# Mixing's value, gate and half u and the memory's keys by token with 512 weight columns moving, roots by token, and a filler of 32 bytes

## The chip, the cores and the metric

The kernel runs on one core of one Trainium2 chip. The metric is the device time of one execution in microseconds (us). The kernel before took 2160.71 us, the median of 3 runs (2157.63 to 2162.42).

## The reference

One layer of a streaming encoder in float32, 256 tokens of width D = 2048, with 256 memory tokens:

```
x += 1/2 * (silu(h W_gate) * (h W_up)) W_out          h = rms(x), hidden width 5632
p = rms(x) @ W_mix_in -> [value | gate | u | v]       1024 columns each
  A = silu(LayerNorm(causal depthwise conv31(value * sigmoid(gate))))
  B = gelu(u) * (masked W_s (LN gelu(v)) + b)         over chunks of 128 positions, 8 groups
x += concat(rms(A), rms(B)) @ W_mix_out
x += softmax(q k^T / sqrt(512)) v ... @ W_o           4 heads; q from rms(x), k and v from rms(mem)
x += 1/2 * SwiGLU_2(rms(x));  out = rms(x)
```

All products of weights with activations need nearly float32 precision. The norms' root of a token is a factor per token, so it can be applied after the product with the weights.

## The kernel before

**Precision.** Every weight and activation is split in two parts of type float32r, hi and lo (x = hi + lo). A product is three matmuls: hi with hi, hi with lo and lo with hi. `weights` (lines 97 to 109) brings a chunk of 128 x 1024 weights: one DMA of 512 KB on SP's queue into a `raw` tile (4 buffers), a copy on ScalarE that makes hi (line 104) and a subtraction on VectorE that makes lo (line 105), both into an `hl` tile (3 buffers). Each chunk is 4 KB in every partition.

**Two shapes of product.** Activations lie by feature: x_hl is [128 features, 16 feature tiles, hi and lo, 256 tokens]. In `gemm_t` with joint=True (`product_joint`, lines 120 to 125) a weight tile of 128 x 128 is the stationary operand and 256 tokens move: three matmuls with 256 columns for each weight tile; the result is by feature. In `gemm_n` (lines 152 to 169) 128 tokens of x_hl are the stationary operand and 512 weight columns move, six matmuls for each 128 x 512 weights (two token halves), and the result is by token, in two PSUM tiles acc[0] and acc[1]. So 128 x 1024 weights are 24 matmuls with 256 columns or 12 with 512. PSUM has 6 buffers of `acc` and 2 of `aux`.

**Stages.** First FFN: `swiglu_in` (lines 267 to 308) in 11 groups of 512 hidden columns by token, whose results are turned to features with transposes on PE (`turn`, 4 transposes a call, two calls a group) into hA (tiles 0 to 15, in the pool `big`) and hB (tiles 16 to 43, in the pool `ffn1`); its output by `gemm_n` in 4 groups (44 feature tiles each: 16 of hA, 28 of hB), turned by `joins` (lines 371 to 386), which adds to x and makes the next x_hl. Mixing (lines 456 to 528): value and gate for 8 column tiles by `gemm_t`, then the half v by `gemm_n`; the memory's keys (16 tiles, lines 586 to 588) and the half u (8 tiles, lines 592 to 599) by `gemm_t`; the memory's values by `gemm_n`. Then mixing's output, attention, and the second FFN like the first, with x2 for the result by token and a last output group in another order (lines 836 to 849).

**Order.** Small work goes beside the matmuls: `put` appends parts with a cost to `later`, and `beside(per)` after each chunk takes parts until a budget of `per` us is spent (lines 80 to 90). The 8 x 31 taps of the convolution (0.4 us of budget each) are such parts, as are the preparation of the memory's activations m_hl and the gate's norms. The argument `between` is a list of calls, here turns, of which one is taken after a chunk, from feature tile k0 = 4 on. The program's order is then rearranged for each engine by the planner of the TileContext, which simulates the engines.

**Roots.** `rms_rows` (line 215) gives the root of each token along the free axis in all partitions, by a product with ones; `rms_cols` (line 220) gives it by token in partitions. r_x and r_m are by rows: r_x multiplies value, gate and u, r_m multiplies the attention's scores over the memory tokens (line 669). r_t and r_mt are by token.

**Where tiles lie.** Pools follow one another in each partition, with tiles rounded up to 32 bytes. The pool `big` holds x_hl, hA, m_hl, y_hl and o_hl in two buffers that begin at bytes 20,032 and 52,800 (313 x 64 and 825 x 64). The pool `st` of small tiles takes 12,256 bytes from 132,672 to 144,928. There `ffn1`, later `mid` and the second FFN's pool begin, each with its first tile: hB begins at 144,928 (2264 x 64 + 32) in both FFNs. `st` holds r_m and r_x with 1,024 bytes each.

## Time and profile before

| | us |
|---|---|
| median of 3 runs | 2160.71 |
| lowest and highest | 2157.63, 2162.42 |
| the profiled execution | 2159.74 |
| its span, first to last instruction | 2157.9 |
| TensorE (PE) busy | 2137.3 |
| VectorE (DVE) busy | 1301.8 |
| ScalarE (ACT) busy | 996.7 |
| mean granted TensorE clock | 0.999 |

The span is cut into stages by what PE reads: value and gate from 750.6 to 846.0 us, the half v to 889.5, the keys to 985.2, the half u to 1031.3, the memory's values to 1120.2, mixing's output to 1209.2. PE's instructions overlap: the next one starts long before the listed end of the last. So a stream of matmuls is measured from start to start, a listed duration (0.28 or 0.39 us) is not what it costs, and an engine that is busy 99% may still do the same work in less time.

### The profile page before, as it was taken

The page shows a single profiled execution, that of the slowest core. Times are in us where ns is not written, and L with a number is a line of the kernel's source. Part 1 is how long each engine was busy: PE and PEld are TensorE (multiplying, and loading weights), DVE is VectorE, ACT ScalarE, POOL GpSimd, SP SyncE. Part 2 cuts the span into 40 slices and gives each one's busy share as a digit, 9 for nine tenths or more (in the row PEclk, how much of TensorE's full clock was granted, in tenths as well). Part 3 has the DMA queues.
Part 4 walks back from the last instruction along what each step waited for, and adds up shares of the span by engine and source line. Part 5 has one row for each costly group of instructions (what it writes and reads, how often), then busy time and mean ns, then how long its engine had stood idle before and what let it go on. Part 6 is the DMA issues. An engine that isn't in the chain of part 4 may idle for free.

```text
span 2157.9 us, 27852 instructions
## 1 busy us (share of the span) xinstructions
PE 2137.3 (99%) x10844; PEld 1814.8 (84%) x10844; DVE 1301.8 (60%) x1673; ACT 996.7 (46%) x1232; POOL 13.3 (1%) x23
## 2 busy tenths in 40 slices
PE   8999999999999999999999999999999999999998
PEld 6788888888888899999888888888888888888886
DVE  4655445555554489888897666776644545444444
ACT  5544444444444454534575454544444444443443
POOL 0000000000000000000000000000000000000000
PEclk9999999999999999999999999999999999999999
DMA  8766666666666676656666653666666666666664
GB/s 272 228 186 193 188 191 181 194 188 190 186 186 186 186 243 195 186 176 184 187 185 194 187 157 114 200 194 185 189 192 188 192 182 192 191 206 192 188 192 149
DMA packets 113605, 409.92 MB, mean 190 GB/s; under 512 B 12736, under 2 KB 12864, under 8 KB 113344
## 3 DMA queue, kind: packets, MB, share of 16 engines
q1 hardware_dynamic: 113184, 407.35, 62.7%
q8 instruction: 85, 1.39, 0.3%
q10 hardware_dynamic: 288, 0.79, 0.1%
q14 instruction: 48, 0.39, 0.0%
HBM read 405.99 MB, written 2.10 MB: 189 GB/s over the span
## 4 chain that ended last, share of the span: by engine, by line
PE 95%; DMA 2%; DVE 1%; ACT 1%; issue 1%; SPq 0%; DVEq 0%; ACTq 0%
PE acc L262 14%; PE acc L258 14%; PE acc L259 14%; PE acc L165 9%; PE acc L163 9%; PE acc L164 9%; PE acc L117 8%; PE acc L118 4%; PE acc L123 3%; PE acc L124 3%; PE acc L125 3%; PE acc L832 1%; PE acc L834 1%; PE acc L833 1%; PE aux L288 1%; DMA raw<-in_x 1%
## 5 line engine op out<-in xcount | busy, mean ns | idle before, releaser
L105 DVE TENSOR_TENSOR hl<-raw,hl 128x1024 fp32r<-128x1024 f32 x751 | 916.4, 1222 | 783.0 <-ACT hl L104 780.7
L104 ACT CAST hl<-raw 128x1024 fp32r<-128x1024 f32 x751 | 783.0, 1046 | 1014.2 <-PE acc L262 506.9
L259 PE MATMUL acc<-hl,x_hl 128*128 128x512 f32 x1408 | 446.7, 392 | 0.5 <-DVE hl L105 0.5
L262 PE MATMUL acc<-hl,x_hl 128*128 128x512 f32 x1408 | 441.6, 390 | 0.0
L258 PE MATMUL acc<-hl,x_hl 128*128 128x512 f32 x1408 | 395.3, 393 | 9.6 <-ACT hl L104 8.0
L258 PEld LDWEIGHTS acc<-hl,x_hl 128*128 128x128 f32 x1408 | 261.7, 188 | 62.5 <-ACT hl L104 8.4
L262 PEld LDWEIGHTS acc<-hl,x_hl 128*128 128x128 f32 x1408 | 264.9, 188 | 55.5
L259 PEld LDWEIGHTS acc<-hl,x_hl 128*128 128x128 f32 x1408 | 263.2, 188 | 54.9 <-DVE hl L105 1.0
L165 PE MATMUL acc<-hl,hB 128*128 128x512 f32 x392 | 155.1, 396 | 0.0
L164 PE MATMUL acc<-hl,hB 128*128 128x512 f32 x392 | 154.5, 394 | 0.0
L163 PE MATMUL acc<-hl,hB 128*128 128x512 f32 x392 | 139.2, 395 | 0.0
L125 PE MATMUL acc<-x_hl,hl 128*128 128x256 f32 x384 | 108.7, 285 | 0.3
L123 PE MATMUL acc<-x_hl,hl 128*128 128x256 f32 x384 | 108.7, 284 | 0.2 <-ACT hl L104 0.2
L124 PE MATMUL acc<-x_hl,hl 128*128 128x256 f32 x384 | 108.4, 283 | 0.0
L117 PE MATMUL acc<-x_hl,hl 128*128 128x512 f32 x256 | 90.6, 396 | 0.0
L117 PE MATMUL acc<-o_hl,hl 128*128 128x512 f32 x256 | 89.0, 394 | 0.0
L117 PE MATMUL acc<-y_hl,hl 128*128 128x512 f32 x256 | 89.0, 394 | 0.0
L165 PEld LDWEIGHTS acc<-hl,hB 128*128 128x128 f32 x392 | 73.6, 188 | 18.1
L164 PEld LDWEIGHTS acc<-hl,hB 128*128 128x128 f32 x392 | 73.5, 188 | 17.9
L163 PEld LDWEIGHTS acc<-hl,hB 128*128 128x128 f32 x392 | 73.4, 187 | 17.9
L164 PE MATMUL acc<-hl,hA 128*128 128x512 f32 x224 | 87.7, 391 | 0.0
L165 PE MATMUL acc<-hl,hA 128*128 128x512 f32 x224 | 87.3, 390 | 0.0
(225 smaller groups left out, 2644.6 us busy)
## 6 DMA issues: line engine op xcount, KB each, us to landing
raw<-in_ffn_w_in SPq DMA_DIRECT2D x352, 512.0 KB, 3.7
raw<-in_ffn_w_out SPq DMA_DIRECT2D x176, 512.0 KB, 3.7
raw<-in_w_mix_in SPq DMA_DIRECT2D x48, 512.0 KB, 4.5
raw<-in_w_k SPq DMA_DIRECT2D x32, 512.0 KB, 4.1
raw<-in_w_v SPq DMA_DIRECT2D x32, 512.0 KB, 4.3
raw<-in_w_mix_out SPq DMA_DIRECT2D x32, 512.0 KB, 4.5
raw<-in_w_q SPq DMA_DIRECT2D x32, 512.0 KB, 3.9
raw<-in_w_o SPq DMA_DIRECT2D x29, 512.0 KB, 4.5
```

Of the source, the lines that this page charges most:

```text
L104: nc.scalar.copy(out=hl[:, 0, :size], in_=raw[:, :size])
L105: newest[0] = nc.vector.tensor_tensor(out=hl[:, 1, :size], in0=raw[:, :size], in1=hl[:, 0, :size].bitcast(F32), op=ALU.subtract)
L117: nc.tensor.matmul(acc, lhsT=w_hi, rhs=x_hl, start=first, stop=False, skip_group_check=True)
L123: nc.tensor.matmul(d, lhsT=w_hi, rhs=x_hl[:, 0], start=first, stop=False, skip_group_check=True)
L124: nc.tensor.matmul(d, lhsT=w_hi, rhs=x_hl[:, 1], start=False, stop=False, skip_group_check=True)
L125: nc.tensor.matmul(d, lhsT=w_lo, rhs=x_hl[:, 0], start=False, stop=last, skip_group_check=True)
L163: nc.tensor.matmul(acc[t], lhsT=x[:, 0, s], rhs=hi[:, k], start=k0 + k == 0, stop=False)
L164: nc.tensor.matmul(acc[t], lhsT=x[:, 0, s], rhs=lo[:, k], start=False, stop=False)
L165: nc.tensor.matmul(acc[t], lhsT=x[:, 1, s], rhs=hi[:, k], start=False, stop=k0 + k == nk - 1)
L258: nc.tensor.matmul(acc[t][g], lhsT=x[:, 0, s], rhs=hi[:, c], start=first, stop=False)
L259: nc.tensor.matmul(acc[t][g], lhsT=x[:, 0, s], rhs=lo[:, c], start=False, stop=False)
L262: nc.tensor.matmul(acc[t][g], lhsT=x[:, 1, s], rhs=hi[:, c], start=False, stop=last)
```

## The change

Value and gate are now laid out side by side: a group of 512 moving columns has 256 of the value and 256 of the gate (4 groups). The half u (2 groups) and the keys (4 groups) also go through `gemm_n` with 512 columns. Their results by token are finished by token (sigmoid, gelu or a plain copy with the token's root as the scale) into a tile o, and turned to features by `turning`, a helper made out of `joins`: 4 transposes into one `aux` tile and a function that takes it from there. The turns are taken between chunks, from k0 = 4 on, in value and gate from k0 = 2 on. The last turns of the first FFN's output are no longer taken at once but between the first chunks of value and gate. The budget `per` is 1.35 in all these groups (1.0, 1.3 and 0.9 before). load_gate and memory_parts stand ahead of a group instead of behind a column tile. r_x by rows and r_m by rows go; the keys carry the memory's root r_mt, and the scores go to the maximum and the exponential without a product. An unused tile of 32 bytes, to_64, is the first in `st`.

```diff
@@ -73,6 +73,9 @@
     pa = ctx.enter_context(tc.tile_pool(name="pa", bufs=2, space=bass.MemoryType.PSUM))
 
 
+    st.tile([P, 8], F32, name="to_64")
+
+
     later = deque()
     budget = [0.0]
     newest = [None]
@@ -149,7 +152,7 @@
                     between.pop(0)()
         return accs
 
-    def gemm_n(w, x_hl, per=0.0, between=None):
+    def gemm_n(w, x_hl, per=0.0, between=None, after=4):
 
         acc = [ps.tile([P, 2, 256], F32, name="acc").rearrange("p a b -> p (a b)") for _ in range(2)]
         nk = w.shape[1]
@@ -163,7 +166,7 @@
                     nc.tensor.matmul(acc[t], lhsT=x[:, 0, s], rhs=hi[:, k], start=k0 + k == 0, stop=False)
                     nc.tensor.matmul(acc[t], lhsT=x[:, 0, s], rhs=lo[:, k], start=False, stop=False)
                     nc.tensor.matmul(acc[t], lhsT=x[:, 1, s], rhs=hi[:, k], start=False, stop=k0 + k == nk - 1)
-            if between and k0 >= 4:
+            if between and k0 >= after:
                 between.pop(0)()
             beside(per)
         return acc
@@ -244,6 +247,18 @@
             )
         gained(x_hl, f, xT[:, f], col(norm, f))
         square_into(ss, xT[:, f], f == 0)
+
+    def turning(o, c, sink):
+
+        def go():
+            tp = pa.tile([P, 2, T], F32, name="aux")
+            for k in range(2):
+                for t in range(2):
+                    nc.tensor.transpose(
+                        out=tp[:, k, t * P:(t + 1) * P], in_=o[:, t, c + k * P:c + (k + 1) * P], identity=ident
+                    )
+            sink(tp)
+        return go
 
 
     G = 512
@@ -361,22 +376,15 @@
         put(1.4, *[memory_squares(c) for c in range(4)])
         turns = swiglu_in(pool, x_hl, lambda: r_x, a["ffn1_w_in"], hA, hB, first_group, 1.4)
         finish()
-        r_m = rms_rows(sm, D, "r_m")
         r_mt = rms_cols(sm, D, "r_mt")
 
 
         x_hl = gained_tile("mix_norm")
         ss = st.tile([P, T], F32, name="ss", bufs=2)
 
-        def joins(f, o, c):
-
-            def go():
-                tp = pa.tile([P, 2, T], F32, name="aux")
-                for k in range(2):
-                    for t in range(2):
-                        nc.tensor.transpose(
-                            out=tp[:, k, t * P:(t + 1) * P], in_=o[:, t, c + k * P:c + (k + 1) * P], identity=ident
-                        )
+        def joins(f):
+
+            def go(tp):
                 nc.vector.scalar_tensor_tensor(
                     out=xT[:, f:f + 2], in0=tp, scalar=0.5, in1=xT[:, f:f + 2], op0=ALU.mult, op1=ALU.add
                 )
@@ -390,9 +398,7 @@
             o = pool.tile([P, 2, G], F32, name="h", bufs=2)
             for t in range(2):
                 nc.scalar.copy(out=o[:, t], in_=acc[t])
-            turns += [joins(4 * n + 2 * i, o, 2 * i * P) for i in range(2)]
-        while turns:
-            turns.pop(0)()
+            turns += [turning(o, 2 * i * P, joins(4 * n + 2 * i)) for i in range(2)]
 
 
     with tc.tile_pool(name="mid", bufs=1) as mid:
@@ -453,28 +459,33 @@
                         nc.vector.tensor_tensor(out=mu, in0=mu, in1=y[:, j], op=ALU.add)
                 return go
 
-            for j in range(NCT):
-                ws = [a["w_mix_in"][j], a["w_mix_in"][NCT + j]]
-                if j == 0:
-                    accs = ahead(ws, lambda k: x_hl[:, k], per=1.0, joint=True)
-                    r_x = rms_rows(ss, D, "r_x")
+            def gated_input(n):
+
+                def go(tp):
+                    for i in range(2):
+                        j = 2 * n + i
+                        pad = pool.tile([P, PAD + T], F32, name="pad", bufs=6)
+                        half = pool.tile([P, T], F32, name="half", bufs=2)
+                        nc.gpsimd.memset(pad[:, 0:PAD], 0.0)
+                        nc.scalar.copy(out=pad[:, PAD:], in_=tp[:, i])
+                        put(0.4, *[tap(j, pad, i, half) for i in range(TAPS)])
+                        put(0.7, conv_sum(j, half))
+                return go
+
+            for n in range(NCT // 2):
+                load_gate(n)
+                later.appendleft((1.6, memory_parts(n)))
+                acc = gemm_n(a["w_mix_vg"][n], lambda k: x_hl[:, k], per=1.35, between=turns, after=2)
+                if n == 0:
                     r_t = rms_cols(ss, D, "r_t")
-                else:
-                    accs = [gemm_t(w, lambda k: x_hl[:, k], per=1.0, joint=True) for w in ws]
-                tv = ev.tile([P, T], F32, name="tg")
-                tg = ev.tile([P, T], F32, name="tu")
-                nc.vector.tensor_tensor(out=tg, in0=accs[1][:, 0], in1=r_x, op=ALU.mult)
-                nc.scalar.activation(out=tg, in_=tg, func=AF.Sigmoid)
-                nc.vector.tensor_tensor(out=tv, in0=accs[0][:, 0], in1=r_x, op=ALU.mult)
-                pad = pool.tile([P, PAD + T], F32, name="pad", bufs=6)
-                half = pool.tile([P, T], F32, name="half", bufs=2)
-                nc.gpsimd.memset(pad[:, 0:PAD], 0.0)
-                nc.vector.tensor_tensor(out=pad[:, PAD:], in0=tv, in1=tg, op=ALU.mult)
-                put(0.4, *[tap(j, pad, i, half) for i in range(TAPS)])
-                put(0.7, conv_sum(j, half))
-                if j < 4:
-                    load_gate(j)
-                    later.appendleft((1.6, memory_parts(j)))
+                o = pool.tile([P, 2, T], F32, name="o", tag="o", bufs=2)
+                for t in range(2):
+                    tg = ev.tile([P, T], F32, name="tu")
+                    nc.scalar.activation(out=tg, in_=acc[t][:, T:], func=AF.Sigmoid, scale=r_t[:, t:t + 1])
+                    nc.vector.scalar_tensor_tensor(
+                        out=o[:, t], in0=acc[t][:, :T], scalar=r_t[:, t:t + 1], in1=tg, op0=ALU.mult, op1=ALU.mult
+                    )
+                turns.append(turning(o, 0, gated_input(n)))
 
 
             c_state = {}
@@ -522,7 +533,7 @@
 
             vs = pool.tile([P, 2, CC], F32, name="vs")
             for n in range(2):
-                acc = gemm_n(a["w_mix_v"][n], lambda k: x_hl[:, k], per=1.35)
+                acc = gemm_n(a["w_mix_v"][n], lambda k: x_hl[:, k], per=1.35, between=turns)
                 for t in range(2):
                     nc.scalar.activation(
                         out=vs[:, t, n * 512:(n + 1) * 512], in_=acc[t], func=AF.Gelu, scale=r_t[:, t:t + 1]
@@ -583,20 +594,35 @@
             put(3.2, conv_rms)
 
 
-            for f in range(KD):
-                acc = gemm_t(a["w_k"][f], lambda k: m_hl[:, k], per=1.3, joint=True)
-                nc.scalar.copy(out=kT[:, f], in_=acc[:, 0])
+            def keys(f):
+                return lambda tp: nc.scalar.copy(out=kT[:, f:f + 2], in_=tp)
+
+            for n in range(HEADS):
+                acc = gemm_n(a["w_k"][n], lambda k: m_hl[:, k], per=1.35, between=turns)
+                o = pool.tile([P, 2, G], F32, name="o", tag="o", bufs=2)
+                for t in range(2):
+                    nc.scalar.activation(out=o[:, t], in_=acc[t], func=AF.Copy, scale=r_mt[:, t:t + 1])
+                turns += [turning(o, 2 * i * P, keys(4 * n + 2 * i)) for i in range(2)]
 
 
             sg = st.tile([P, T], F32, name="sg")
-            for j in range(NCT):
-                tu = ev.tile([P, T], F32, name="tu")
-                acc = gemm_t(a["w_mix_in"][2 * NCT + j], lambda k: x_hl[:, k], per=0.9, joint=True)
-                nc.vector.tensor_tensor(out=tu, in0=acc[:, 0], in1=r_x, op=ALU.mult)
-                nc.scalar.activation(out=tu, in_=tu, func=AF.Gelu)
-                z = g_state["z"][:, j].rearrange("p n i -> p (n i)")
-                nc.vector.tensor_tensor(out=z, in0=z, in1=tu, op=ALU.mult)
-                square_into(sg, z, j == 0)
+
+            def gating(f):
+                def go(tp):
+                    z = g_state["z"][:, f:f + 2].rearrange("p j n i -> p j (n i)")
+                    nc.vector.tensor_tensor(out=z, in0=z, in1=tp, op=ALU.mult)
+                    for i in range(2):
+                        square_into(sg, z[:, i], f + i == 0)
+                return go
+
+            for n in range(2):
+                acc = gemm_n(a["w_mix_u"][n], lambda k: x_hl[:, k], per=1.35, between=turns)
+                o = pool.tile([P, 2, G], F32, name="o", tag="o", bufs=2)
+                for t in range(2):
+                    nc.scalar.activation(out=o[:, t], in_=acc[t], func=AF.Gelu, scale=r_t[:, t:t + 1])
+                turns += [turning(o, 2 * i * P, gating(4 * n + 2 * i)) for i in range(2)]
+            while turns:
+                turns.pop(0)()
 
             y_hl = big.tile([P, KD, 2, T], F32R, name="y_hl", tag="S")
 
@@ -666,14 +692,13 @@
                     for d in range(KH):
                         product_joint(acc, q_hl[:, d, 0, s], q_hl[:, d, 1, s], k_hl[:, d], d == 0, d == KH - 1)
                     e = pool.tile([P, M], F32, name="e", bufs=4)
-                    nc.vector.tensor_tensor(out=e, in0=acc[:, 0], in1=r_m, op=ALU.mult)
                     mx = st.tile([P, 1], F32, name="mx", bufs=2)
                     sm = st.tile([P, 1], F32, name="sum", bufs=2)
-                    nc.vector.reduce_max(out=mx, in_=e, axis=AX.X)
+                    nc.vector.reduce_max(out=mx, in_=acc[:, 0], axis=AX.X)
                     nc.vector.tensor_scalar(
                         out=mx, in0=mx, scalar1=r_t[:, t:t + 1], scalar2=-1.0, op0=ALU.mult, op1=ALU.mult
                     )
-                    nc.scalar.activation(out=e, in_=e, func=AF.Exp, scale=r_t[:, t:t + 1], bias=mx, accum_out=sm)
+                    nc.scalar.activation(out=e, in_=acc[:, 0], func=AF.Exp, scale=r_t[:, t:t + 1], bias=mx, accum_out=sm)
                     nc.vector.reciprocal(out=sm, in_=sm)
                     nc.vector.tensor_scalar(out=e, in0=e, scalar1=sm, scalar2=None, op0=ALU.mult)
                     pr.append(e)
@@ -878,11 +903,13 @@
         a[name] = np.ascontiguousarray(w.transpose(3, 1, 0, 2, 4).reshape(F // 512, P, KD, 1024))
     a["ffn1_w_out"] = _tiled(g["ffn1_w_out"][0], 512)
     a["ffn2_w_out"] = _tiled(g["ffn2_w_out"][0], 512)
-    a["w_mix_in"] = _tiled(g["w_mix_in"][0][:, :3 * CC], P)
+    w = g["w_mix_in"][0][:, :2 * CC].reshape(KD, P, 2, CC // 256, 256)
+    a["w_mix_vg"] = np.ascontiguousarray(w.transpose(3, 1, 0, 2, 4).reshape(CC // 256, P, KD, 512))
+    a["w_mix_u"] = _tiled(g["w_mix_in"][0][:, 2 * CC:3 * CC], 512)
     a["w_mix_v"] = _tiled(g["w_mix_in"][0][:, 3 * CC:], 512)
     a["w_mix_out"] = _tiled(g["w_mix_out"][0], P)
     a["w_q"] = _tiled(g["w_q"][0], P)
-    a["w_k"] = _tiled(g["w_kv"][0][:, :D], P)
+    a["w_k"] = _tiled(g["w_kv"][0][:, :D], 512)
     a["w_v"] = _tiled(g["w_kv"][0][:, D:], 512)
     a["w_o"] = _tiled(g["w_o"][0], P)
     a["sgu_wT"] = np.ascontiguousarray(g["sgu_w"][0].transpose(2, 0, 1))
```

## Rows read from the trace of the kernel before

**Rows 1.** The page: busy time by engine (part 1) and the chain by engine (part 4).

```profile
PE 2137.3 (99%) x10844; PEld 1814.8 (84%) x10844; DVE 1301.8 (60%) x1673; ACT 996.7 (46%) x1232; POOL 13.3 (1%) x23
...
PE 95%; DMA 2%; DVE 1%; ACT 1%; issue 1%; SPq 0%; DVEq 0%; ACTq 0%
```

**Rows 2.** Stretches: length; PE, PEld, DVE, ACT, POOL busy; PEclk, DMA share, GB/s.

```profile
750.60:846.00 95.40, 94.94 (x784) 94.08 (x783) 81.91 (x149) 48.30 (x69) 1.05 (x8) 1.00 0.70 222
846.00:889.50 43.50, 43.50 (x194) 36.04 (x193) 39.86 (x71) 20.05 (x21) 0.12 (x1) 1.00 0.63 191
889.50:985.20 95.70, 95.70 (x802) 95.66 (x802) 81.41 (x147) 42.87 (x56) 0.00 (x0) 1.00 0.59 177
...
1209.20:1338.70 129.50, 128.42 (x798) 114.45 (x797) 83.32 (x149) 66.75 (x119) 0.00 (x0) 1.00 0.49 144
```

**Rows 3.** Waits of PE: who was waited for, total us, times, longest.

```profile
PE acc L258 <- ACT hl L104: 8.0, 2, 7.6
PE acc L258 <- ACT h L274: 1.6, 1, 1.6
```

**Rows 4.** PE's timeline (start us, us): the half u's first matmul and its successor stage.

```profile
985.18 0.28 PE L123 MATMUL acc<-x_hl,hl 128*128 128x256 f32 x1
...
1031.26 0.40 PE L163 MATMUL acc<-hl,m_hl 128*128 128x512 f32 x1
```

**Rows 5.** PE's timeline: first matmul of the other half, first one of the keys.

```profile
845.99 0.40 PE L163 MATMUL acc<-hl,x_hl 128*128 128x512 f32 x1
...
889.54 0.28 PE L123 MATMUL acc<-m_hl,hl 128*128 128x256 f32 x1
```

**Rows 6.** PE's groups by form: names, shapes, count, busy us, mean ns, idle before.

```profile
L123 PE MATMUL acc<-x_hl,hl 128*128 128x256 f32 x384 | 108.7, 284 | 0.2 <-ACT hl L104 0.2
```

**Rows 7.** PE's timeline: first transposes in two successive groups of the first FFN.

```profile
107.08 0.38 PE L288 MATMUL aux<-ident,h 128*128 128x128 f32 x2
...
151.57 0.38 PE L288 MATMUL aux<-ident,h 128*128 128x128 f32 x2
```

**Rows 8.** PE's timeline: mixing's root by rows, then its root by token.

```profile
766.13 0.59 PE L212 MATMUL aux<-ss,ones 128*128 128x256 f32 x2
766.56 0.50 PE L223 MATMUL aux<-ones,ss 128*128 128x1 f32 x4
```

**Rows 9.** PE's timeline, second FFN's output: where hA begins, hB, hA again.

```profile
1965.96 0.39 PE L163 MATMUL acc<-hl,hA 128*128 128x512 f32 x1
...
1987.73 0.39 PE L163 MATMUL acc<-hl,hB 128*128 128x512 f32 x1
...
2026.92 0.62 PE L163 MATMUL acc<-hl,hA 128*128 128x512 f32 x2
```

**Rows 10.** PE's groups by form with hB as the stationary operand.

```profile
L165 PE MATMUL acc<-hl,hB 128*128 128x512 f32 x392 | 155.1, 396 | 0.0
...
L833 PE MATMUL acc<-hl,hB 128*128 128x512 f32 x40 | 15.8, 395 | 0.0
```

**Rows 11.** ScalarE's groups by form, 750.6 to 1120.2 us.

```profile
L621 ACT ACTIVATE vv<-acc,r_mt 128x512 f32<-128x512 f32 x7 | 4.8, 684 | 1.7 <-PE acc L165 1.7
```

**Rows 12.** VectorE's groups by form, 750.6 to 1120.2 us.

```profile
L105 DVE TENSOR_TENSOR hl<-raw,hl 128x1024 fp32r<-128x1024 f32 x128 | 156.6, 1223 | 40.8 <-ACT hl L104 39.2
L442 DVE SCALAR_TENSOR_TENSOR y<-pad,pv,y 128x256 f32<-128x256 f32 x120 | 57.6, 480 | 0.0
```

**Rows 13.** VectorE's groups by form, 1209.2 to 1415.1 us.

```profile
L669 DVE TENSOR_TENSOR e<-aux,r_m 128x256 f32<-128x256 f32 x8 | 3.4, 421 | 2.4 <-PE aux L125 2.3
```

**Rows 14.** Timeline of SP's queue (DMA issues) where mixing begins.

```profile
736.37 11.53 SPq L101 DMA_DIRECT2D raw<-in_w_mix_in  x5
...
754.57 0.33 SPq L408 DMA_DIRECT2D wT<-in_sgu_wT  x1
```

**Rows 15.** Timeline of ScalarE and of VectorE: the first value and gate are finished.

```profile
774.29 1.28 ACT L467 ACT_TABLE_LOAD   x1
...
778.70 0.42 DVE L472 TENSOR_TENSOR pad<-tg,tu 128x256 f32<-128x256 f32 x1
```

## The prediction

> **What bounds the kernel now.** The page comes first: TensorE is busy 99% of the 2157.9 us and holds 95% of the chain that ended last [rows 1]. The profiled execution took 2159.74 us, 1.84 us more than its span, and lies 0.97 us under the median of the runs, 2160.71 us. I work on 2159.74 and shift the answer to the median. The second view is the busy time by stage [rows 2]: from 750.6 to 985.2 us (value and gate, the gate's other half, keys) PE is busy in all but 0.46 us, while VectorE reaches 92% and ScalarE 51% at most. The third is PE's waits [rows 3]: 8.0 us at the start of the program and 1.6 us behind the first gated group are nearly all of them. So in the stages that change the reader should not look for a wait to remove; their time is the number of PE instructions times the distance from one start to the next. (The mean durations on the page overlap and are no such distance.) The fourth view is therefore PE's timeline, read for starts alone, with the groups by form for counts.
>
> **Narrow matmuls become wide ones.** The stage of the half u before is pure: 384 matmuls with 256 columns moving from 985.18 to 1031.26 us, 46.08 us, 120.0 ns each [rows 4]. The stage of the other half, the same x_hl through gemm_n, is pure in the new form: 192 matmuls with 512 columns from 845.99 to 889.54 us, 43.55 us, 226.8 ns each [rows 5]. The change touches three lines of 384 with x_hl [rows 6] and the same three of 256 with m_hl, 1920 narrow ones, whose weights and products stay the same; 960 wide ones do the work: 1920 x 120.0 = 230.4 us against 960 x 226.8 = 217.7 us. **Term 1: -12.7 us**, all on the path. Wide ones at 233.3 ns (the slowest steady stream of that form, below) would leave -6.4; I take 226.8 because it was measured on one of the very tiles.
>
> [...] The rows differ by 2 x 120.0 - 226.8 = 13.2 ns at a granted clock of 1.00 [rows 2, 4, 5]. [...]
>
> **Turning back.** Results by token are turned to features by calls of `turning`: 4 for the gated value, 8 for keys, 4 for u, so 16 calls of 4 transposes. The FFN's groups carry the price: the first transposes of two successive groups, 192 wide matmuls and 8 transposes apart, start 151.57 - 107.08 = 44.49 us from each other [rows 7]; 43.55 of it are the matmuls, which leaves 0.94 us for 8, 0.47 us a call. **Term 2: +7.5 us** on the path. Each transpose at its listed half of 0.38 us for a pair, nothing overlapped, would make it 64 x 0.19 = +12.2, the upper end; 0 would be the lower, if PE had gaps to fill, which it has not.
>
> **Roots.** The two roots by rows go. Each is one f32 product with ones, two records on PE, 766.13 to 766.56 us, 0.43 us [rows 8]. **Term 3: -0.9 us.** The roots by token r_t and r_mt stay. The root chains on VectorE lie beside PE, and their end gives nothing.
>
> **The filler.** The tiles of pool st push what lies behind them to byte 144,928, which is 32 past a multiple of 64; there hB begins, the larger part of both FFNs' hidden tile. hA, x_hl and m_hl in pool big begin on multiples of 64. After the change st loses 2 x 1,024 bytes and gains 32, and hB begins at 142,912, a multiple. The trace has one line with the same moving tile on both: with hA as the stationary operand 96 matmuls from 1965.96 to 1987.73 us, 226.8 ns each; with hB 168 from 1987.73 to 2026.92 us, 233.3 ns [rows 9]. Shapes and code differ in nothing but the place. With hB there are three lines of 392 and three of 40 [rows 10], and from the last group's held weights 4 chunks x 2 tiles x 2 token halves x 3 lines = 48 more, 1344 in all. If the 32 bytes are the cause, **term 4: 1344 x 6.5 = -8.7 us**; if something else about the place is, 0. Nothing here would make hB slower than now. I take -8.7, since the two places differ in the very thing that the filler changes.
>
> [...]
>
> **What lies beside,** costed at nothing, with its cover:
> - VectorE: per weight chunk of 1024 columns one split of 1.22 us, and 1.35 us of budget for conv taps in all these groups (1.0 before in value and gate, 1.3 in keys, 0.9 in u). A tap is listed at 0.48 us [rows 12] and budgeted at 0.4. The stage at 846 us ran at that pace with the same 12 x 226.8 ns = 2.72 us of PE a chunk: VectorE 39.86 of 43.50 us busy, PE without a gap [rows 2]. New products and old ones are alike in number or fewer. Without that cover 3.4 taps x 0.48 + 1.22 = 2.84 us a chunk would exceed PE by 0.12 us in up to 88 chunks, 10.6 us: the upper end.
> - ScalarE: in keys 8 evictions and 8 copies of 128x512 at the 0.68 us of the values' eviction [rows 11], 10.9 us at most, where it is busy 42.87 of 95.70 us [rows 2].
> - Attention: the 8 products with r_m (0.42 us each [rows 13]) leave the chain from scores to exponential. PE idles 1.08 us in that whole stage [rows 2], which bounds the gain; the maximum and the exponential now read PSUM and hold its bank longer, which could cost as much. I take 0, between -1 and +1.
> - SP: the loads of load_gate now stand ahead of a group's weights, and the wT load follows the FFN's last transposes, which now come after the group's second and third chunk. Before, five weight loads of the coming stage were issued ahead of wT [rows 14]; the four raw buffers cover as many chunks. If the fifth chunk's load waits behind wT until the third chunk is done (750.6 + 3 x 2.72 = 759 us) and behind its 2 MB, at 222 GB/s [rows 2] 9 us, it lands at 768 instead of 761: PE loses up to 7 us once. The weights' layout still gives 4 KB a partition and load.
> - New waits: a call's transposes stand in PE's queue behind a chunk (k0 of 4 and more; 2 in value and gate), and all later matmuls behind them. They need the eviction: in the first group before, it took from the table load at 774.29 to the finished pad at 779.12, 4.8 us, 1.28 of it the table load [rows 15]. The cover is two chunks, 5.4 us. The FFN's groups run this way with no wait but the first [rows 3, 7].
>
> **Sum.** -12.7 + 7.5 - 0.9 - 8.7 = -14.8 us: 2159.74 goes to 2144.9, the median 2160.71 to **2146 us**. Its own range with the small unknowns (attention, a few short waits) is 2140 to 2151.
>
> **Rivals.**
> 1. The filler changes nothing; another property of the place slows hB. For it: the narrow stream shows 120.0 ns from start to finish, whatever it loads [rows 4]. Against: one line, two tiles, nothing else different. 2146 + 8.7 = 2154.7 us. [...]
> 2. VectorE or SP sets the pace in mixing: VectorE at 92% with PE's chunk down from 24 x 120.0 = 2.88 to 2.72 us, or the blocked load. 7 to 10.6 us: 2153 to 2157 us, 2155 in the middle. Against: the stage at 846 us.
> 3. Slower: the turns stall PE. Each of the 16 calls may wait in the middle of PE's queue for root, table load, eviction and product. From 14.8 / 16 = 0.9 us a call nothing is left; if the 4.8 us chain grew to 6.7 us, 1.3 us past its cover, the sum would be +6 us: 2167 us. For it: the first gated group of the FFN did wait 1.6 us [rows 3], and Sigmoid, Gelu and Sqrt share ScalarE here. Against: the FFN's later groups of the same shape don't wait.
> 4. It doesn't do what it says: the wide matmuls run at hB's 233.3 ns here. 2146 + 6.2 = 2152 us. Against: rows 5, on x_hl itself.
>
> **How the numbers follow.** The forecast has 0.70, rival 1 0.09, rival 2 0.10, rival 3 0.05, rival 4 0.03; 0.03 is left for a gain beyond it. About 0.2%, 4.3 us, is what a measurement of this kernel can tell from no change: faster means under 2156.4, slower over 2165.0. The forecast, the gain beyond it, rival 4, most of rival 1 and half of rival 2 lie under 2156.4: faster 0.88; the rest of rivals 1 and 2 and the mild end of rival 3 make same 0.08; slower 0.04. The range reaches from 2139 (the forecast's lower end and 1 us from attention) to 2155, which takes in rivals 1 and 4 and the milder half of rival 2.
>
> **What would show it.** Term 1: 226.8 ns between the starts of value and gate, keys and u, where 120.0 stood. Term 2: 64 more transposes, about 0.12 us each, and no PE wait ahead of them. Term 4: hB's segment of 168 matmuls takes 38.1 us instead of 39.19, eight times; were it still 39.2, rival 1 holds. A PE wait for an eviction at the transposes would show rival 3; one for a weight's split, or for raw loads near 760 us, rival 2. Over 2156 us the sum is wrong in at least one of the large terms 1, 2 and 4.

## The result, and the profile after

The changed kernel took 2146.28 us (median of 4 runs, 2145.18 to 2147.76) where the kernel before took 2160.39 us (median of 4, 2157.63 to 2162.42): a ratio of 0.9935, 95% interval 0.9920 to 0.9949, so 14.1 us less. Predicted were 2146.0 us and a change of -14.8 us. The profiled execution of the changed kernel took 2147.76 us, the longest of the four, with a span of 2146.0 us.

First the page of the changed kernel, busy time and the chain by engine, which answer to [rows 1]:

```profile
PE 2124.5 (99%) x9944; PEld 1770.8 (83%) x9944; DVE 1284.9 (60%) x1627; ACT 1005.5 (47%) x1234; POOL 13.3 (1%) x23
...
PE 95%; DMA 2%; DVE 1%; ACT 1%; issue 1%; SPq 0%; DVEq 0%; ACTq 0%
```

TensorE has 900 instructions less: 1920 narrow matmuls became 960 wide ones (-960), 64 transposes came, 4 records of two roots went. Its share and the chain have not moved, so TensorE still sets the pace. The waits of PE, which answer to [rows 3] (who was waited for, total us, times, longest):

```profile
PE acc L273 <- ACT hl L107: 8.4, 4, 7.1
PE acc L273 <- ACT h L289: 1.6, 1, 1.6
PE acc L167 <- DVE hl L108: 0.8, 2, 0.5
PE acc L126 <- ACT p_hl L115: 0.6, 1, 0.6
```

The transposes (line 257) are in none of them: nothing waits at the new turns. The third row is new, two short waits for VectorE's lo part at 771.5 and 774.8 us, in value and gate (0.2 us in a second execution of the changed kernel): all that came of rival 2.

The windows of the changed kernel by stage, which answer to [rows 2] (length; PE, PEld, DVE, ACT, POOL busy; PEclk, DMA share, GB/s): value, gate and the half v with the last hB matmuls of the FFN ahead of them; keys; the half u; the memory's values; mixing's output.

```profile
709.00:882.50 173.50, 172.72 (x774) 142.24 (x773) 136.30 (x226) 86.75 (x111) 1.18 (x9) 1.00 0.67 212
882.50:976.00 93.50, 93.50 (x442) 78.00 (x441) 82.33 (x151) 46.18 (x54) 0.00 (x0) 1.00 0.60 181
976.00:1021.40 45.40, 45.40 (x209) 37.52 (x208) 41.80 (x75) 22.95 (x28) 0.00 (x0) 1.00 0.61 185
1021.40:1111.30 89.90, 89.90 (x401) 74.33 (x400) 76.23 (x120) 61.68 (x94) 0.00 (x0) 1.00 0.61 187
1111.30:1201.80 90.50, 90.50 (x514) 78.44 (x513) 62.51 (x91) 45.20 (x64) 0.00 (x0) 1.00 0.57 187
```

PE has no gap in keys, u, the memory's values and the output, and 0.78 us of gaps in the first stretch; VectorE reaches 92% in u and has not become the bound. Two of the same stretches in the kernel before, the first and the last:

```profile
711.40:889.50 178.10, 177.64 (x1143) 161.62 (x1142) 138.92 (x232) 83.47 (x104) 1.18 (x9) 1.00 0.67 207
...
1120.20:1209.20 89.00, 89.00 (x514) 77.76 (x513) 69.98 (x108) 49.91 (x73) 0.00 (x0) 1.00 0.63 192
```

No line of the last one was touched by the change, and it has the same 514 matmuls, but it is 1.5 us longer now. That was not foreseen; the last part of this text comes back to it.

PE's timeline of the changed kernel where u begins and ends (answers to [rows 4]), and the groups by form in between (count, busy us, mean ns, idle before):

```profile
975.98 0.39 PE L166 MATMUL acc<-hl,x_hl 128*128 128x512 f32 x1
...
1021.41 0.39 PE L166 MATMUL acc<-hl,m_hl 128*128 128x512 f32 x1
```

```profile
L166 PE MATMUL acc<-hl,x_hl 128*128 128x512 f32 x64 | 22.7, 396 | 0.0
...
L257 PE MATMUL aux<-ident,o 128*128 128x128 f32 x16 | 2.7, 272 | 0.0
```

u takes 1021.41 - 975.98 = 45.43 us: 192 wide matmuls at the 226.8 ns of [rows 5], 43.55 us, and 16 transposes, which are 4 calls (two of the keys' last head, two of u) at 0.47 us, 1.88 us. The sum is 45.43 us.

PE's timeline of the changed kernel in the second FFN's output, which answers to [rows 9]:

```profile
1957.17 0.39 PE L166 MATMUL acc<-hl,hA 128*128 128x512 f32 x1
...
1978.93 0.39 PE L166 MATMUL acc<-hl,hB 128*128 128x512 f32 x1
...
2017.01 0.39 PE L166 MATMUL acc<-hl,hA 128*128 128x512 f32 x1
```

96 matmuls with hA take 21.76 us as before; 168 with hB take 38.08 us instead of 39.19, 226.7 ns each: hB now runs like hA.

The whole, stage by stage, in us, from the starts of the first matmuls on PE's timelines (one profiled execution each):

| stage | before | after | |
|---|---|---|---|
| first FFN, products in | 495.41 | 496.78 | +1.37; in a second execution of the changed kernel 494.65 |
| first FFN, three segments of hB | 3 x 39.19 | 3 x 38.08 | -3.33 |
| fourth hB segment, value, gate, half v | 178.10 | 173.46 | -4.64; second execution 172.67 |
| keys | 95.64 | 93.49 | -2.15 |
| half u | 46.08 | 45.43 | -0.65 |
| memory's values | 88.92 | 89.90 | +0.98: the last two calls of u fall here (0.94) |
| mixing's output | 88.99 | 90.44 | +1.45; second execution 90.43 |
| second FFN, products out | 253.87 | 249.62 | -4.25: four segments of hB |

Queries, attention's output and the second FFN's products in differ by 0.3 us at most between these two executions. In the second execution of the changed kernel attention's output took 101.60 us instead of 100.31; the last part explains it.

### The profile page after: what moved, and what is told of

Read it like the earlier page. It is cut to its first block, busy times and chain, and to the rows that moved or that the text cites. A ratio compares the mean times of both kernels' runs of the same rounds, so it can differ in the third digit from the quotient of the medians.

```text
span 2146.0 us, 26016 instructions
## 1 busy us (share of the span) xinstructions
PE 2124.5 (99%) x9944; PEld 1770.8 (83%) x9944; DVE 1284.9 (60%) x1627; ACT 1005.5 (47%) x1234; POOL 13.3 (1%) x23
## 4 chain that ended last, share of the span: by engine, by line
PE 95%; DMA 2%; DVE 1%; ACT 1%; issue 1%; SPq 0%; DVEq 0%; ACTq 0%
PE acc L274 14%; PE acc L277 14%; PE acc L273 14%; PE acc L167 12%; PE acc L168 12%; PE acc L166 12%; PE acc L120 8%; PE acc L121 4%; PE acc L857 1%; PE acc L859 1%; PE acc L858 1%; DMA raw<-in_x 1%; PE aux L303 1%; DMA raw<-in_memT 1%; PE aux L257 0%
## 5 line engine op out<-in xcount | busy, mean ns | idle before, releaser
L274 PE MATMUL acc<-hl,x_hl 128*128 128x512 f32 x1408 | 446.9, 392 | 0.6 <-DVE hl L108 0.5
L277 PE MATMUL acc<-hl,x_hl 128*128 128x512 f32 x1408 | 441.3, 390 | 0.0
L273 PE MATMUL acc<-hl,x_hl 128*128 128x512 f32 x1408 | 395.4, 393 | 10.0 <-ACT hl L107 8.4
L167 PE MATMUL acc<-hl,hB 128*128 128x512 f32 x392 | 152.7, 389 | 0.0
L168 PE MATMUL acc<-hl,hB 128*128 128x512 f32 x392 | 152.6, 389 | 0.0
L166 PE MATMUL acc<-hl,hB 128*128 128x512 f32 x392 | 136.7, 389 | 0.0
L167 PE MATMUL acc<-hl,x_hl 128*128 128x512 f32 x256 | 100.6, 393 | 0.8 <-DVE hl L108 0.8
L167 PE MATMUL acc<-hl,m_hl 128*128 128x512 f32 x256 | 100.4, 392 | 0.0
L168 PE MATMUL acc<-hl,m_hl 128*128 128x512 f32 x256 | 100.2, 392 | 0.0
L168 PE MATMUL acc<-hl,x_hl 128*128 128x512 f32 x256 | 99.8, 390 | 0.0
L166 PE MATMUL acc<-hl,m_hl 128*128 128x512 f32 x256 | 91.3, 393 | 0.0
L166 PE MATMUL acc<-hl,x_hl 128*128 128x512 f32 x256 | 90.2, 392 | 0.0
```

Source lines behind the costliest of these rows:

```text
L166: nc.tensor.matmul(acc[t], lhsT=x[:, 0, s], rhs=hi[:, k], start=k0 + k == 0, stop=False)
L167: nc.tensor.matmul(acc[t], lhsT=x[:, 0, s], rhs=lo[:, k], start=False, stop=False)
L168: nc.tensor.matmul(acc[t], lhsT=x[:, 1, s], rhs=hi[:, k], start=False, stop=k0 + k == nk - 1)
L273: nc.tensor.matmul(acc[t][g], lhsT=x[:, 0, s], rhs=hi[:, c], start=first, stop=False)
L274: nc.tensor.matmul(acc[t][g], lhsT=x[:, 0, s], rhs=lo[:, c], start=False, stop=False)
L277: nc.tensor.matmul(acc[t][g], lhsT=x[:, 1, s], rhs=hi[:, c], start=False, stop=last)
```

## Experiments

All kernels are edits of the changed kernel except where the kernel before is named. They ran in three groups, each on one chip together with the kernel before, whose medians were 2159.05, 2159.11 and 2158.53 us. Each ratio is to the kernel before of the same group, and kernels of different groups are compared by their ratios or by their stages.

### Without the 32 bytes

```
-    st.tile([P, 8], F32, name="to_64")
```

> The changed kernel without the 32 byte tile, so that hB begins 32 past a multiple of 64 again. Theory (the 32 bytes decide how fast hB is loaded): the 1344 matmuls with hB go back from 226.8 to 233.3 ns, a segment of 168 from 38.1 to 39.2 us, +8.7 us against the changed kernel: about 2155 us, 5 to 6 us under the kernel before. Rival (another property of hB's place, as its distance from pool big): hB lies 2 KB lower than before, segments stay at 38.1 us, 2146 us.

2154.03 us (9 runs), ratio 0.9977 (0.9967 to 0.9987). PE's timeline in the second FFN's output:

```profile
1959.72 0.39 PE L163 MATMUL acc<-hl,hA 128*128 128x512 f32 x1
...
1981.49 0.39 PE L163 MATMUL acc<-hl,hB 128*128 128x512 f32 x1
...
2020.68 0.39 PE L163 MATMUL acc<-hl,hA 128*128 128x512 f32 x1
```

The hB segment is back at 39.19 us. Without the filler the change is worth 5.0 us.

### The 32 bytes alone, in the kernel before

```
     pa = ctx.enter_context(tc.tile_pool(name="pa", bufs=2, space=bass.MemoryType.PSUM))
+    st.tile([P, 8], F32, name="to_64")
```

> The kernel before with nothing but the 32 byte tile. Theory: hB's segments 38.1 instead of 39.2 us, 8 x 1.1 = -8.7 us: about 2152 us. Rival (the gain of hB in the changed kernel comes from the 2 KB that st lost, not from the 32 bytes): no difference, 2160 us.

2150.03 us (5 runs), ratio 0.9961 (0.9949 to 0.9974): -9.0 us. PE's timeline of hB's segment:

```profile
1983.82 0.39 PE L164 MATMUL acc<-hl,hB 128*128 128x512 f32 x1
...
2021.90 0.39 PE L164 MATMUL acc<-hl,hA 128*128 128x512 f32 x1
```

38.08 us with nothing else changed. The two halves of the change add up: -5.0 - 9.0 = -14.0, and the whole gave -14.1, or -13.0 when it was measured again (below).

### Each new transpose twice

```
+                    for _ in range(times):
+                        nc.tensor.transpose(
+                            out=tp[:, k, t * P:(t + 1) * P], in_=o[:, t, c + k * P:c + (k + 1) * P], identity=ident
+                        )
```

> The changed kernel with each of the 64 new transposes issued twice. Theory (they lie on the path at 0.117 us from start to start): +7.5 us against the changed kernel, about 2154 us. Rival (PE has slack in these stages and they are hidden): 2146 us. Rival (each costs its listed 0.19 us): +12.2 us, 2158 us.

2152.85 us (7 runs), ratio 0.9974 (0.9963 to 0.9986); against the changed kernel's ratio of 0.9935 that is 0.0039, some 8 us. PE's timeline of u, and the doubled transposes in it:

```profile
977.62 0.39 PE L166 MATMUL acc<-hl,x_hl 128*128 128x512 f32 x1
...
1024.88 0.39 PE L166 MATMUL acc<-hl,m_hl 128*128 128x512 f32 x1
```

```profile
L258 PE MATMUL aux<-ident,o 128*128 128x128 f32 x32 | 4.8, 272 | 0.0
```

u grew from 45.43 to 47.26 us, 1.83 us for 16 more transposes, 0.114 us each. Keys grew by 2.69 us (6 calls), the memory's values by 0.84 (2 calls), value, gate and v by 1.2 to 2.0 (4 calls, by which execution is subtracted): 6.6 to 7.4 us for 64, where 7.5 stand in the prediction. A transpose in u's stream cost its own 0.114 us and no wait.

### Each wide matmul as two halves

```
+                    for c0, n in [(0, 256), (256, 256)] if halves else [(0, 512)]:
+                        c = slice(c0, c0 + n)
...
+                            acc[t][:, c], lhsT=x[:, 0, s], rhs=hi[:, k, c], start=begin, stop=False, skip_group_check=True
```

in value and gate, keys and u. The layout and the turns stay; the three products follow each other as before, first for one half of the columns and then for the other.

> The changed kernel in which every matmul with 512 columns moving of value and gate, keys and u is two with 256, in the same order, turns as they are: term 1 alone undone. Theory (a matmul costs its columns and a fixed distance): 1920 x 120.0 against 960 x 226.8 ns, +12.7 us against the changed kernel, about 2159 us, level with the kernel before, u's stage 45.4 + 2.5 = 47.9 us. Rival (the gain came from less work around the matmuls, not from the width): 2146 us.

2157.07 us (11 runs), ratio 0.9992 (0.9983 to 1.0001): level with the kernel before. PE's timeline of u and one line of it:

```profile
982.41 0.28 PE L170 MATMUL acc<-hl,x_hl 128*128 128x256 f32 x1
...
1030.22 0.40 PE L170 MATMUL acc<-hl,m_hl 128*128 128x512 f32 x1
```

```profile
L170 PE MATMUL acc<-hl,x_hl 128*128 128x256 f32 x128 | 36.4, 286 | 0.0
```

u takes 47.81 us; less 1.88 for the turns that is 45.93 us for 384 matmuls, 119.6 ns each, the pace of [rows 4] with the operands' roles exchanged. So the 120.0 ns belonged to the width of 256, not to which operand was held. (PE and PEld count alike on the pages, 10844 each before and 9944 each after, so every matmul has a weight load of its own: half the width is also twice the loads, and the runs don't part the two.) The stages grew by 2.38 (u), 4.79 (keys) and 3.4 to 4.2 us (value and gate), 10.6 to 11.4 together; by the ratios it is 12 us.

### The changed kernel again

> The changed kernel once more, as the reference on this chip and for what repeats from one execution to the next. Theory: 2146 us, mixing's output again 90.4 us (353 ns for a pair of one 512 and one 256 wide matmul, against 347 in most of that stage of the kernel before), while the opening of the first FFN, where loads land differently, moves by up to 1.5 us. Rival: both are chance, and mixing's output comes back to 89.0 us.

2146.14 us (4 runs, 2145.49 to 2146.97), ratio 0.9938 (0.9925 to 0.9952): -13.0 us in this group. The first FFN's products in took 494.65 us where the first profile had 496.78: 2.1 us by which two executions of one kernel differ, so the +1.37 us of that stage is no effect of the change. Mixing's output took 90.43 us again: its 1.45 us repeat.

### Which address counts

The prediction put term 4 down to hB's own start, 32 past a multiple of 64 bytes. Four kernels move tiles. The weights' tile hl (here the moving operand) and the activations (hA, hB, x_hl, m_hl, the stationary ones) stand in the same space, so a filler placed early moves all that lies behind it. In the kernel before and in the changed one hl begins behind the two buffers of `big` and the four of raw, at byte 52,800 + 32,768 + 4 x 4,096 = 101,952 (1593 x 64).

First the tile moved to the front of everything:

```
     const = ctx.enter_context(tc.tile_pool(name="const", bufs=1))
+    const.tile([P, 8], F32, name="to_64")
...
-    st.tile([P, 8], F32, name="to_64")
```

> The changed kernel with the 32 byte tile in the first pool (const) instead of st: x_hl, hA, m_hl and the weights' tiles begin 32 past a multiple of 64, hB still on one. Theory (a load of the stationary operand from 32 past costs 6.5 ns behind a 512 wide matmul): hB stays at 226.8 ns, the 6528 wide matmuls with x_hl, hA and m_hl go to 233.3, +42 us, about 2189 us. Rival (hB was slow for being far behind in the partition): hA and x_hl stay at 226.8, 2146 us.

2154.29 us (10 runs), ratio 0.9979 (0.9970 to 0.9988). x_hl, m_hl, hA and hl now begin 32 past a multiple, hB on one. PE's timeline in the second FFN's output:

```profile
1960.71 0.39 PE L164 MATMUL acc<-hl,hA 128*128 128x512 f32 x1
...
1982.48 0.39 PE L164 MATMUL acc<-hl,hB 128*128 128x512 f32 x1
...
2021.67 0.39 PE L164 MATMUL acc<-hl,hA 128*128 128x512 f32 x1
```

A miss, and the instructive one: hA, now 32 past, is fast (21.77 us), and hB, now on a multiple, is slow (39.19 us). The stationary operand's start by itself does not decide it.

Then the tile between the activations' pool and the weights' pools:

```
     big = ctx.enter_context(tc.tile_pool(name="big", bufs=2))
+    gap = ctx.enter_context(tc.tile_pool(name="gap", bufs=1))
+    gap.tile([P, 8], F32, name="to_64")
...
-    st.tile([P, 8], F32, name="to_64")
```

> The changed kernel with a second 32 byte tile between pool big and the weights' pools and st's tile kept: only the weights' tiles (raw, hl), ev and st's first tiles move to 32 past a multiple; hB, x_hl, hA stay on one... hB because st's tile then pads from 32 past. Theory (only the stationary operand's address counts): the 7872 wide matmuls, where hl moves, stay at 226.8 ns unless their stationary operand moved too; the 768 pairs of mixing's output, queries and attention's output, where hl is stationary, cost up to 6.6 ns more each, +2 to +5 us, 2148 to 2151 us. Rival (the moving operand's address counts as well): +50 us, 2196 us.

(Where that text places the 32 bytes otherwise than the diff, the diff is what ran: the one tile, moved. hl begins 32 past; x_hl, m_hl, hA and hB on multiples.) 2193.08 us (4 runs), ratio 1.0156 (1.0142 to 1.0170).

```profile
1998.06 0.40 PE L165 MATMUL acc<-hl,hA 128*128 128x512 f32 x1
...
2020.46 0.40 PE L165 MATMUL acc<-hl,hB 128*128 128x512 f32 x1
...
2059.66 0.40 PE L165 MATMUL acc<-hl,hA 128*128 128x512 f32 x1
```

Both are slow: 22.40 us for 96 with hA and 39.20 for 168 with hB, 233.3 ns each. There are 7872 wide matmuls of this kind in the program; the 46.9 us that this kernel is longer than the changed one are 6.0 ns for each. Another miss for the stationary operand alone. With the run before it says that what counted in these streams is how the two operands' starts stand to each other.

That theory was then put to a test with its own number: the filler in st stays and another one goes ahead of the weights, so that hl and hB are both 32 past and the rest is on multiples.

```
     big = ctx.enter_context(tc.tile_pool(name="big", bufs=2))
+    gap = ctx.enter_context(tc.tile_pool(name="gap", bufs=1))
+    gap.tile([P, 8], F32, name="gap_32")
```

> The changed kernel with st's 32 byte tile kept and one more ahead of the weights' pools: the moving hl tiles and the stationary hB begin 32 past a multiple of 64, x_hl, hA and m_hl on one. New theory (what counts is the distance between the stationary and the moving operand's address, modulo 64: 0 is fast, 32 is slow): hB at 226.8 ns, x_hl, hA and m_hl at 233.3, 8.7 us less than the run with hB on a multiple, about 2184 us. Rival (a moving operand 32 past a multiple is slow by itself, and all tiles 32 past together were fast for another reason): hB stays at 233.3, about 2193 us.

2182.84 us (4 runs), ratio 1.0110 (1.0094 to 1.0125).

```profile
1989.90 0.39 PE L168 MATMUL acc<-hl,hA 128*128 128x512 f32 x1
...
2012.29 0.39 PE L168 MATMUL acc<-hl,hB 128*128 128x512 f32 x1
...
2050.38 0.39 PE L168 MATMUL acc<-hl,hA 128*128 128x512 f32 x1
```

It holds: hB, 32 past like hl, is fast (38.09 us), and hA, on a multiple, is slow (22.39).

What distance counts, with hl on a multiple of 64, and hB 16 past it in the first FFN and 48 past it in the second:

```
+    def hidden(pool, past):
+        size = (KF - KD) * 2 * T
+        flat = pool.tile([P, size + 16], F32R, name="hB")
+        return flat[:, past // 4:past // 4 + size].rearrange("p (k two t) -> p k two t", two=2, t=T)
...
+        hB = hidden(pool, 16)
...
+        hB = hidden(pool, 48)
```

> The changed kernel with the first FFN's hB begun 16 bytes past a multiple of 64 and the second FFN's 48, hl on multiples. Theory a (the distance modulo 64, as a scale): 16 and 48 lie between 226.8 and 233.3 ns. Theory b (the two operands must lie alike modulo 64): both 233.3, +8.7 us, about 2155 us. Theory c (only modulo 32 matters in some way and 16 and 48 are alike): the same value for both FFNs, whatever it is.

2151.06 us (6 runs), ratio 0.9963 (0.9950 to 0.9975). PE's timeline of an hB segment of the first and of the second FFN:

```profile
524.38 0.39 PE L166 MATMUL acc<-hl,hB 128*128 128x512 f32 x1
...
562.46 0.39 PE L166 MATMUL acc<-hl,hA 128*128 128x512 f32 x1
...
1979.31 0.40 PE L166 MATMUL acc<-hl,hB 128*128 128x512 f32 x1
...
2018.50 0.39 PE L166 MATMUL acc<-hl,hA 128*128 128x512 f32 x1
```

16 past is fast (38.08 us), 48 past is slow (39.19). None of the theories named ahead of the run gives just this. All pairs seen so far, starts counted from a multiple of 64 bytes:

| stationary | moving | ns a wide matmul | seen in |
|---|---|---|---|
| 0 | 0 | 226.8 | before, changed kernel |
| 32 | 0 | 233.3 | before (hB) |
| 32 | 32 | 226.8 | filler ahead of all (hA); both past (hB) |
| 0 | 32 | 233.3 | filler ahead of all (hB); ahead of the weights (both) |
| 16 | 0 | 226.7 | this run |
| 48 | 0 | 233.3 | this run |

Two descriptions fit these six pairs. By the first, the matmuls took 226.7 or 226.8 ns where both operands began in the same 32-byte half of a stretch of 64 bytes, and 233.3 where they didn't. By the second, they took 226.7 or 226.8 where the stationary one began less than 32 bytes past the moving one, modulo 64, and 233.3 elsewhere. Both were formed after the last run, and no pair that was tried tells them apart (32 with 16 would); that either holds for other pairs, and why the chip does so, was not shown. They describe streams of wide matmuls alone: in mixing's output, where wide and narrow ones alternate, two of these kernels had hl 32 past and y_hl on a multiple, and one took 353.3 ns a pair, the other 346.7, no more than 226.8 + 120.0.

### All hi products of a chunk, then all lo products

This is for the 1.45 us of mixing's output, where each weight tile is held for a matmul with 512 columns and another one for 256, in turn.

```
+                product_hi(acc, hi[:, k], x_hl(k0 + k), first and k == 0)
+        for k in range(0 if joint else kk):
+            product_lo(acc, lo[:, k], x_hl(k0 + k), last and k == kk - 1)
```

> The changed kernel with another order in the stages where 512 and 256 wide matmuls alternate (mixing's output, queries, attention's output): in a chunk first the eight 512 wide ones, then the eight 256 wide ones. Theory (a uniform stream has 226.8 and 120.0 ns, so a pair costs 346.8, and the 353 comes from the alternation alone): mixing's output 88.8 instead of 90.4 us, the three stages together about -3 us, 2143 us. Rival (the pair's cost is that of the two loads whatever the order): 2146 us.

2144.37 us (5 runs, 2142.82 to 2145.48), ratio 0.9929 (0.9916 to 0.9941). PE's timeline of the stage:

```profile
1109.09 0.39 PE L120 MATMUL acc<-y_hl,hl 128*128 128x512 f32 x1
...
1198.44 0.40 PE L120 MATMUL acc<-x_hl,hl 128*128 128x512 f32 x1
```

89.35 us: 1.1 us of the 1.45 came back, not all of it. The three stages together took 295.1 us, where the two executions of the changed kernel took 296.2 and 297.5; 3 us less had been forecast. That alternation alone makes 353 ns is not so either, since some alternating stretches run at 346.7 (last part). It is the fastest kernel of all that ran; beside the changed kernel on the same chip (2146.14) the gain is 1.8 us. The intervals of the two ratios overlap, so only its sign in the medians is seen.

## Why the prediction was right, and where its reasons were not

**What bounds it.** Right. TensorE holds 95% of the chain as before, the stages that changed have no gap but the 0.78 us above, and each experiment moved them by a number of instructions times a pitch (the distance from one start to the next).

**Term 1, -12.7 us: right.** The wide pitch on the path is 226.8 ns in u (45.43 us to the hundredth). Cut in two it costs 10.6 to 11.4 us by the stages, 12 by the ratios; at the 119.6 ns measured there the term would be -11.9. The rest of the 12.7 is within what the executions differ by (2.1 us in the first FFN's products in).

**Term 2, +7.5 us: right.** 0.47 us a call is confirmed in u and in the memory's values, and doubling the transposes cost 6.6 to 7.4 us by the stages and some 8 by the ratios. The price from the FFN, where the same 8 transposes lie in the same kind of stream, carried over.

**Term 3, -0.9 us: the instructions went** (the 4 records in the count above); its size is too small to be told apart in a stage.

**Term 4, -8.7 us: right in size, wrong in reason.** Alone it measured -9.0, and by the pitch 8 segments x 1.11 = 8.9. But the prediction said "32 past a multiple of 64" of hB, as if that place were slow. It was slow (233.3 ns) beside a moving operand that begins on a multiple; with hl 32 past, the same place was fast (168 in 38.09 us, 226.7 ns each) and the multiple slow (96 in 22.39 us, 233.2). The price, 6.5 ns, belongs to a pair of tiles, and the prediction gave it to one. It was luck that the moving tiles lay on multiples in both kernels, so that hB's own start decided. With the same 32 bytes ahead of the weights its rule would have forecast the same gain, since all activations and hB are on multiples there, and the kernel was 34 us slower than the one before (2193.08 against 2159.11). By the runs, beside a moving operand on a multiple of 64, stationary starts 0 and 16 past one are fast (226.8 and 226.7 ns) and 32 and 48 past one slow (233.3).

**What lies beside.** VectorE's and SP's cover held but for 0.8 us of waits, and so did ScalarE's. Attention was costed at 0 within 1 us. From the first query to the end of attention's output it took 205.9 us before and 205.8 in the first execution of the changed kernel; in the second it took 207.1, and the 1.3 us more lie in the pace of attention's output, not in the scores.

**What was missed.** Mixing's output, in no term, became 1.45 us longer. The measured -14.1 us holds it, so the terms gave some -15.5 against the -14.8 predicted; the second measurement, -13.0 us, leaves -14.4 for them. Both lie within 1 us of the forecast, but the interval of either measurement is some 3 us to each side. That 2146 us was met to 0.3 us is in part luck: something that was not forecast weighed against the terms.

**The rivals.** Rival 1 (the filler changes nothing, 2154.7 us): out, by the filler alone; the kernel without it came to 2154.03. Rival 2 (VectorE or SP sets the pace): 0.8 us of the 7 to 10.6. (Its upper end counts 88 chunks, but 1920 narrow matmuls at 24 a chunk are 80, 9.6 us; the forecast doesn't change by it.) Rival 3 (the turns stall PE, 2167 us): out, no wait at line 257, and doubling them cost only their own length. Rival 4 (the wide ones run at 233.3 ns): out where it was looked for; the run with the filler ahead of the weights shows the state it feared, and that a placement decides it.

## What to carry to other kernels

Where TensorE has no gaps, count instructions and take the distance between starts from a pure stretch of the same form in the same trace; here the price of an added call (0.47 us) could then be taken from another stage with the same stream, and the sum of such terms came within 2 us of what was measured. When one line shows two paces with two tiles (226.8 and 233.3 ns here), look at the starts of both operands before blaming one, and test a filler by moving it, not only by taking it out. After any change of layout or order, compare the stages that were not touched as well, and in more than one execution.

## What was not expected of the hardware

In these streams of nothing but matmuls with 512 columns, each cost 6.5 ns more (233.3 for 226.8) when the starts of its two operands stood to each other as in the slow rows of the table above; over all of the kernel with the filler ahead of the weights it was 6.0. Whether a stream with 256 columns pays such a price was not tried: in the stream of [rows 4], at 120.0 ns, and in the halved one, at 119.6, both operands began on multiples of 64. So the even pace of [rows 4], which the prediction's rival 1 counted for itself, said nothing about the place.

The streams that take 512 and 256 columns in turn showed two paces, 353.3 and 346.7 ns a pair. Through each unbroken run of pairs shown here the pace stayed the same. In the changed kernel mixing's output is one run of 256 pairs at 353.3. The kernel before begins the stage at 352.9 as well, but after 35 pairs PE takes two wide matmuls and then two narrow ones (x2 in the lines), and the 219 pairs behind this break run at 346.7:

```profile
1120.18 0.39 PE L117 MATMUL acc<-y_hl,hl 128*128 128x512 f32 x1
...
1132.53 0.64 PE L117 MATMUL acc<-y_hl,hl 128*128 128x512 f32 x2
1133.01 0.40 PE L118 MATMUL acc<-y_hl,hl 128*128 128x256 f32 x2
1133.24 0.40 PE L117 MATMUL acc<-y_hl,hl 128*128 128x512 f32 x1
...
1209.17 0.39 PE L117 MATMUL acc<-x_hl,hl 128*128 128x512 f32 x1
```

219 pairs at 6.6 ns less are 1.45 us, the whole difference. So the same 514 matmuls stand in another order: the changed kernel has no such break in this stage.

The 32 bytes are not the cause: alone they left the break and the 88.99 us, and the changed kernel without them had no break and took 90.44. So did every other kernel with the new value, gate, keys and u, the halved one too, but for two: sorting the products by width gave 349.0 ns a pair (89.35 us), and the kernel with both hl and hB past ran at 346.7 from its first pair on (88.75 us). The relation of the two starts is not the cause either, since the filler ahead of the weights gives this stage's weights the same place as both past does, and left it at 90.44.

Nor does the program alone decide the pace. The last unbroken run of attention's output, 191 pairs, took 346.6 ns a pair in the first execution of the changed kernel and 353.4 in the second. Its first matmul and the one after its end, in the first execution and then in the second:

```profile
1341.32 0.40 PE L120 MATMUL acc<-o_hl,hl 128*128 128x512 f32 x1
...
1407.53 0.39 PE L273 MATMUL acc<-hl,x_hl 128*128 128x512 f32 x1
```

```profile
1338.80 0.40 PE L120 MATMUL acc<-o_hl,hl 128*128 128x512 f32 x1
...
1406.29 0.40 PE L273 MATMUL acc<-hl,x_hl 128*128 128x512 f32 x1
```

In that stage some breaks changed the pace and some left it: in the first execution 12 pairs from 1331.09 us on took 353.3 ns each, the 6 behind the next break 353.3 again, the 6 behind one more 346.7, and the 191 behind a third 346.6. What decides which pace a run takes stays open, and no kernel was run that puts such a break into the changed kernel's mixing output.
